# A hybrid decoder layer: gate and up projections as a 2x2 problem of half products, half of the chunk pairs in seven products, the rest plain

## The chip, the cores and the metric

The kernel runs on one core of one Trainium2 chip. The metric is the device time of one execution in microseconds (us), the median of the runs shown. A core has a matrix engine (TensorE, PE in the rows), three elementwise engines (VectorE or DVE, ScalarE or ACT, GpSimd or POOL), a queue that issues transfers (SyncE, SP), a memory of 128 partitions that the kernel manages (SBUF), and a memory in which products accumulate (PSUM); this kernel uses PSUM as eight tiles of 128x512 floats, called banks here, four for products (`mm`) and four for the rest (`aux`).

## The reference

256 tokens, width 2048, hidden width 5632, 32-bit floats throughout. The change is in the two feed-forward parts:

```python
def swiglu(h, w_gate, w_up, w_down):
    return (jax.nn.silu(h @ w_gate) * (h @ w_up)) @ w_down

x = x + 0.5 * swiglu(rms_norm(x, ffn1_norm[l]), ffn1_w_gate[l], ffn1_w_up[l], ffn1_w_down[l])
...  # gated linear attention beside block attention, w_in and w_out; a memory read with w_q, w_kv, w_o
x = x + 0.5 * swiglu(rms_norm(x, ffn2_norm[l]), ffn2_w_gate[l], ffn2_w_up[l], ffn2_w_down[l])
```

## The kernel before, in words

Every product is made from halves: an operand is split into `hi`, its rounding to the format fp32r, and `lo`, the rest. A product of 128 tokens x 128 rows x 512 columns is then three matmuls into one PSUM bank, hi x hi, hi x lo and lo x hi (L156, L157, L158). Weights stream from memory four 128-row chunks at a time (`load_raw`, 1 MB). `split_unit` splits them two chunks at a time: ScalarE writes `whi` (L130, 128x1024), then VectorE subtracts to get `wlo` (L131, 128x1024). `whi` and `wlo` have three buffers each, so a split waits until TensorE has read the buffer of three splits ago.

The activations `xhi` and `xlo` are the residual, transposed on TensorE (L223), multiplied by the gain (VectorE, L226) and split (ScalarE L228, VectorE L229); 1 / rms of a token is multiplied in behind the product. `Normed.block(j)` does this for one of four column blocks j and two token tiles.

`ffn` goes over 11 column blocks of 512 hidden columns in three runs (4, 4 and 3 blocks). For each column block it makes the gate product, 16 chunks x 2 token tiles x 3 = 96 matmuls into two banks, and the same for up; Silu of the gate (ScalarE, L275), times up (VectorE, L292), then a transpose and a split (L282, L196, L197; 8 transposes) for the down projection, which follows each run (L307 adds it to the residual). What runs behind the products (norms, transposes) is a queue of steps, one taken per product step by `pump()`. The order of instructions on each engine is made from this program by a scheduler before the run, and each engine takes its own in order.

Of the kernel before, what the change touches and what calls it, by code (L numbers as in the profile page):

```python
# [17 lines left out]
P = 128  # L18
# [26 lines left out]
OFF_MV = OFF_MK + BH * DH  # L45


@with_exitstack
def hymba_layer(ctx: ExitStack, tc: tile.TileContext, x, mem, ffn1_norm, ffn1_w_gate, ffn1_w_up,
# [27 lines left out]
    graw = tmp.tile([KC, P], F32, tag="S", name="graw", bufs=6)  # L77
# [12 lines left out]
    def turn_gains(src, dst):  # L90
        n = src.shape[0]
        ps = aux.tile([P, NB], F32, tag="aux", name=nm("aux"))
        nc.tensor.transpose(ps[:, :n], src, ident[:n, :n])
        nc.vector.tensor_copy(dst, ps[:, :n])

    turn_gains(graw, gT1)

    def aux_tile(shape):
        n = 1
        for s in shape[1:]:  # L100
            n *= s
# [7 lines left out]

    def tmp_tile(shape, tag, bufs=2, dtype=F32):  # L110
        return tmp.tile(shape, dtype, tag=tag, name=nm(tag), bufs=bufs)

    def half_kb(shape=(P, NB)):
        return tmp_tile(list(shape), "t2k", 8)
# [3 lines left out]
    def load_raw(k0, c0, w, n=NB, step=4):  # L118
        raw = wp.tile([P, 4, n], F32, tag="raw", name=nm("raw"))
        src = w[k0 * P:(k0 + 4) * P, c0:c0 + n].rearrange("(k p) n -> p k n", p=P)  # L120
        for k in range(0, 4, step):
            nc.sync.dma_start(raw[:, k:k + step, :], src[:, k:k + step, :])
        return raw

    def split_unit(raw, ks, n):
        got = []
        for k in ks:
            hi = wp.tile([P, 2, n], F32R, tag="whi", name=nm("whi"))
            lo = wp.tile([P, 2, n], F32R, tag="wlo", name=nm("wlo"))
            nc.scalar.activation(hi, raw[:, k:k + 2, :], AF.Copy)  # L130
            nc.vector.tensor_tensor(lo, raw[:, k:k + 2, :], hi.bitcast(F32), op=ALU.subtract)  # L131
            got += [(hi[:, i, :], lo[:, i, :]) for i in range(2)]
        return got

    class Block:
        """One [256 tokens, n columns] product; a step takes two or four 128-row chunks of it."""

        def __init__(self, a, w, c0, nk, done, w_k0=0, n=NB):
            self.a, self.w, self.c0, self.nk, self.w_k0, self.n = a, w, c0, nk, w_k0, n
            self.done = done  # L140
            self.ps = [mm.tile([P, NB], F32, tag="mm", name=nm("mm"))[:, :n] for _ in range(NT)]
            self.raw = {}

        def step(self, k0, nk=4):
            u, r = divmod(k0, 4)
            key = id(self.w), self.w_k0 + 4 * u, self.c0
            if u not in self.raw:
                self.raw[u] = ahead.pop(key) if key in ahead else load_raw(*key[1:], self.w, self.n)
            hi, lo = self.a
            ws = split_unit(self.raw[u], range(r, r + nk, 2), self.n)  # L150
            for t in range(NT):
                s = slice(t * P, (t + 1) * P)
                p = self.ps[t]
                for i, (wh, wl) in enumerate(ws):
                    k = k0 + i
                    nc.tensor.matmul(p, hi[:, k, s], wh, start=k == 0, stop=False)  # L156
                    nc.tensor.matmul(p, hi[:, k, s], wl, start=False, stop=False)  # L157
                    nc.tensor.matmul(p, lo[:, k, s], wh, start=False, stop=k == self.nk - 1)  # L158
# [19 lines left out]
    def run_blocks(specs, late=False, gap=4):  # L178
        """With late, the last chunks of the first two blocks come after the others of both."""
# [34 lines left out]
    def sumsq(src, dst):  # L214
        junk = tmp.tile([P, NB], BF16, tag="junk", name=nm("junk"), bufs=1)
# [3 lines left out]
    def norm_block(c, j, t, gi, hi, lo, ss):  # L219
        """Columns j of token tile t (c): transposed, times the gain, split; the squares summed."""  # L220
# [3 lines left out]
        xg = tmp_tile([P, 4, P], "xg")  # L224
# [614 lines left out]
```

## Time and profile before

| | |
|---|---|
| median of 3 runs | 1990.75 us (1989.64 to 1990.9) |
| profiled execution, first to last instruction (span) | 1987.1 us; the page gives no other time for it |
| TensorE matmuls busy | 1973.9 us, 99% |
| VectorE busy | 1075.3 us, 54% |
| ScalarE busy | 918.0 us, 46% |
| bytes moved | 369 MB, mean 186 GB/s |

A busy matmul is drawn as 0.39 us, but one starts every 0.2267 us, so that busy times of lines add up to more than the engine's. Of the elementwise engines, too, one instruction can start a little before the one ahead of it is drawn as ended: the distance of two starts is what an instruction takes from its queue.

### The profile page before, as it was taken

The numbers are of one execution on the slowest core, as the hardware profiler recorded it, in microseconds if no ns is written. First come the engines' busy times: TensorE is split into PE (matmuls) and PEld (weight loads), VectorE is DVE, ScalarE is ACT, GpSimd is POOL, SyncE is SP. The second block draws the span as 40 slices with busy tenths as digits, with TensorE's granted clock in tenths as the row PEclk, the third lists the DMA queues.
The fourth block names the chain that finished last, engine by engine and source line by source line (L and its number), as shares of the span: only waits on it lengthen the run. The fifth ranks groups of instructions, "written<-read, shape, count | busy, mean of one in ns | idle before, by whom it ended". The sixth has DMA issues, their size and how long they took to land.

```text
span 1987.1 us, 22549 instructions
## 1 busy us (share of the span) xinstructions
PE 1973.9 (99%) x9112; PEld 1640.8 (83%) x9112; DVE 1075.3 (54%) x1236; ACT 918.0 (46%) x1112; POOL 19.8 (1%) x52
## 2 busy tenths in 40 slices
PE   8999999999999999999999999999999999999999
PEld 6888888888888888987788889888888888888887
DVE  5454554445544465456665767655544444554444
ACT  5444434444344455635464656544433444434443
POOL 0000000000000000000000000000000000000000
PEclk9999999999999999999999999999999999999999
DMA  7655555555565556554455545555556555556554
GB/s 242 191 191 191 190 191 191 190 191 191 191 191 190 191 170 199 164 191 149 148 167 195 180 158 171 175 190 188 190 190 195 188 190 189 190 195 197 182 189 167
DMA packets 189857, 369.07 MB, mean 186 GB/s; under 512 B 6100, under 2 KB 16552, under 8 KB 189752
## 3 DMA queue, kind: packets, MB, share of 16 engines
q1 hardware_dynamic: 189752, 367.63, 56.7%
q8 instruction: 71, 1.16, 0.3%
q14 instruction: 34, 0.28, 0.0%
HBM read 365.50 MB, written 2.10 MB: 185 GB/s over the span
## 4 chain that ended last, share of the span: by engine, by line
PE 95%; issue 3%; DVE 1%; ACT 1%; DMA 0%; POOL 0%; SPq 0%; POOLq 0%; ACTq 0%
PE mm L157 31%; PE mm L156 30%; PE mm L158 30%; PE aux L282 1%; PE aux L223 1%; DVE wlo L131 0%; DMA x_sb<-in_x_dram 0%; PE aux L767 0%; PE aux L783 0%; PE aux L506 0%; ACT whi L130 0%; PE aux L639 0%; PE aux L585 0%; PE aux L535 0%; PE aux L517 0%
## 5 line engine op out<-in xcount | busy, mean ns | idle before, releaser
L131 DVE TENSOR_TENSOR wlo<-raw,whi 128x1024 fp32r<-128x1024 f32 (+3 forms) x704 | 847.1, 1205 | 852.1 <-ACT whi L130 823.6
L130 ACT ACTIVATE whi<-raw 128x1024 fp32r<-128x1024 f32 (+3 forms) x704 | 733.3, 1043 | 947.4 <-PE mm L158 946.2
L156 PE MATMUL mm<-whi,xhi 128*128 128x512 f32 (+2 forms) x1856 | 719.4, 388 | 0.1
L157 PE MATMUL mm<-wlo,xhi 128*128 128x512 f32 (+2 forms) x1856 | 716.8, 386 | 1.2 <-DVE wlo L131 1.2
L158 PE MATMUL mm<-whi,xlo 128*128 128x512 f32 (+2 forms) x1856 | 716.2, 386 | 0.0
L157 PEld LDWEIGHTS mm<-wlo,xhi 128*128 128x128 f32 x1856 | 348.9, 188 | 70.7 <-DVE wlo L131 3.1
L156 PEld LDWEIGHTS mm<-whi,xhi 128*128 128x128 f32 x1856 | 348.7, 188 | 70.3 <-issue 1.5
L158 PEld LDWEIGHTS mm<-whi,xlo 128*128 128x128 f32 x1856 | 348.7, 188 | 69.0 <-DVE xlo L229 0.2
L158 PE MATMUL mm<-whi,biglo 128*128 128x512 f32 x864 | 336.4, 390 | 0.0
L156 PE MATMUL mm<-whi,bighi 128*128 128x512 f32 x832 | 325.3, 391 | 0.0
L157 PE MATMUL mm<-wlo,bighi 128*128 128x512 f32 x832 | 324.0, 389 | 0.0
L158 PEld LDWEIGHTS mm<-whi,biglo 128*128 128x128 f32 x864 | 162.2, 188 | 33.9
L157 PEld LDWEIGHTS mm<-wlo,bighi 128*128 128x128 f32 x832 | 156.3, 188 | 32.1 <-DVE wlo L131 0.4
L156 PEld LDWEIGHTS mm<-whi,bighi 128*128 128x128 f32 x832 | 156.3, 188 | 31.8
L275 ACT ACTIVATE t2k<-mm,r 128x512 f32<-128x512 f32 x44 | 30.4, 692 | 40.4 <-PE mm L158 40.4
L307 DVE SCALAR_TENSOR_TENSOR x_sb<-mm,x_sb 128x512 f32<-128x512 f32 x48 | 33.0, 688 | 11.1 <-PE mm L158 11.0
L292 DVE SCALAR_TENSOR_TENSOR t2k<-mm,r,t2k 128x512 f32<-128x512 f32 x44 | 32.9, 748 | 8.1 <-PE mm L158 8.0
L197 DVE TENSOR_TENSOR biglo<-aux,bighi 128x512 fp32r<-128x512 f32 (+1 forms) x56 | 34.1, 645 | 0.0
L217 ACT ACTIVATE junk<-x_sb 128x512 bf16<-128x512 f32 x32 | 20.1, 627 | 19.2 <-DVE x_sb L307 9.9
L196 ACT ACTIVATE bighi<-aux 128x512 fp32r<-128x512 f32 (+1 forms) x56 | 28.8, 555 | 0.0
L226 DVE TENSOR_TENSOR xg<-aux,gT 128x512 f32<-128x512 f32 x40 | 25.7, 683 | 0.0
L282 PEld LDWEIGHTS aux<-ident,t2k 128*128 128x128 f32 x176 | 20.5, 141 | 2.9
(170 smaller groups left out, 643.8 us busy)
## 6 DMA issues: line engine op xcount, KB each, us to landing
raw<-in_ffn_w_up_dram SPq DMA_DIRECT2D x88, 1024.0 KB, 5.1
raw<-in_ffn_w_down_dram SPq DMA_DIRECT2D x88, 1024.0 KB, 4.9
raw<-in_ffn_w_gate_dram SPq DMA_DIRECT2D x87, 1024.0 KB, 5.1
raw<-in_w_in_dram SPq DMA_DIRECT2D x40, 1024.0 KB, 5.1
raw<-in_w_out_dram SPq DMA_DIRECT2D x16, 1024.0 KB, 4.9
raw<-in_w_in_dram SPq DMA_DIRECT2D x8, 688.0 KB, 4.2
raw<-in_xattn_w_kv_dram SPq DMA_DIRECT2D x4, 1024.0 KB, 4.9
raw<-in_xattn_w_q_dram SPq DMA_DIRECT2D x4, 1024.0 KB
```

The source lines that it names most:

```text
L130: nc.scalar.activation(hi, raw[:, k:k + 2, :], AF.Copy)
L131: nc.vector.tensor_tensor(lo, raw[:, k:k + 2, :], hi.bitcast(F32), op=ALU.subtract)
L156: nc.tensor.matmul(p, hi[:, k, s], wh, start=k == 0, stop=False)
L157: nc.tensor.matmul(p, hi[:, k, s], wl, start=False, stop=False)
L158: nc.tensor.matmul(p, lo[:, k, s], wh, start=False, stop=k == self.nk - 1)
L196: nc.scalar.activation(hi, src, AF.Copy)
L197: nc.vector.tensor_tensor(lo, src, hi.bitcast(F32), op=ALU.subtract)
L226: nc.vector.tensor_tensor(xg, pt, g[:, :, None].to_broadcast([P, 4, P]), op=ALU.mult)
L275: nc.scalar.activation(sg[b, t], ps[t], AF.Silu, scale=a.rstd[:, t:t + 1])
L282: nc.tensor.transpose(pt[:, i, :], h[t][:, i * P:(i + 1) * P], ident)
L292: nc.vector.scalar_tensor_tensor(h[t], ps[t], a.rstd[:, t:t + 1], sg[b, t], op0=ALU.mult, op1=ALU.mult)
L307: nc.vector.scalar_tensor_tensor(c, ps[t], 0.5, c, op0=ALU.mult, op1=ALU.add)
```

## The change

Let x0, x1 be the two token tiles (the rows of the 2x2 problem) and two neighbouring chunks the inner dimension; the columns are gate and up. For the first four of the eight chunk pairs of a column block (`KINDS` "S"), the eight half products x_t,k times gate_k or up_k are replaced by seven (the scheme of Strassen in Winograd's form): on the weight side VectorE makes four sums of 128x512 (`sa`, `sb`), on the activation side four differences per pair, once for all column blocks. Each of the seven is three matmuls into a bank of its own: `p1`, `r6`, `r7`, `p2`, `r5`, `r3`, `q4`. For the last four pairs ("N") eight plain half products go into four of the same banks, two of them as one with the difference of both token tiles (`dh`, `dl`), as 24 matmuls. `early`, `gates` and `ups` put the banks together on VectorE. So a column block has 4 x 21 + 4 x 24 = 180 matmuls.

With seven banks for `mm` one is left for `aux` in the feed-forward parts. Pools for PSUM and scratch are opened for three phases (`a`, `b`, `c`). Weights come two chunks per transfer (512 KB) into five buffers; `whi` and `wlo` have five buffers in the feed-forward parts. The mixer's constants are made at the start of phase `b`.

```diff
+RAWS = 5
+HIS = 5
+T2K = 7
+KINDS = "SSSSNNNN"
...
-    def load_raw(k0, c0, w, n=NB, step=4):
-        raw = wp.tile([P, 4, n], F32, tag="raw", name=nm("raw"))
...
+    def load_raw(k0, c0, w, n=NB):
+        raw = wp.tile([P, 2, n], F32, tag="raw", name=nm("raw"))
+        nc.sync.dma_start(raw, w[k0 * P:(k0 + 2) * P, c0:c0 + n].rearrange("(k p) n -> p k n", p=P))
+        return raw
...
+    def split_raw(raw, n=NB):
+        bufs = 3 if "mix" in pools else HIS
+        hi, lo = (tmp_tile([P, 2, n], tag, bufs, F32R) for tag in ("whi", "wlo"))
+        split_to(hi, lo, raw)
+        return [(hi[:, i, :], lo[:, i, :]) for i in range(2)]
+
+    def mm3(p, a, w, start, stop):
+        nc.tensor.matmul(p, a[0], w[0], start=start, stop=False)
+        nc.tensor.matmul(p, a[0], w[1], start=False, stop=False)
+        nc.tensor.matmul(p, a[1], w[0], start=False, stop=stop)
...
+        def step(self, q):
...
+            g = take_raw(2 * q, self.c0, self.wg)
+            u = take_raw(2 * q, self.c0, self.wu)
+            if KINDS[q] == "N":
+                gs, us = split_raw(g), split_raw(u)
+                for name, t, ws in (("p2", 0, gs), ("q4", 1, gs), ("r3", None, us), ("r5", 1, us)):
+                    for i, w in enumerate(ws):
+                        x = a.diff(2 * q + i) if t is None else a.plain(t, 2 * q + i)
+                        self.add(name, x, w, i == 1)
+            else:
+                sa, sb = (tmp_tile([P, 2, NB], "st") for _ in range(2))
+                nc.vector.tensor_tensor(sa[:, 0, :], g[:, 0, :], u[:, 0, :], op=ALU.add)
+                nc.vector.tensor_tensor(sa[:, 1, :], u[:, 0, :], u[:, 1, :], op=ALU.add)
+                nc.vector.tensor_tensor(sb[:, 0, :], sa[:, 0, :], u[:, 1, :], op=ALU.add)
+                nc.vector.tensor_tensor(sb[:, 1, :], sb[:, 0, :], g[:, 1, :], op=ALU.add)
+                hu, lu = (tmp_tile([P, NB], tag, 2, F32R) for tag in ("hu", "lu"))
+                gs = split_raw(g)
+                split_to(hu, lu, u[:, 1, :])
+                sums = split_raw(sa) + split_raw(sb)
+                e, o = 2 * q, 2 * q + 1
+                for name, x, w in (("p1", a.plain(0, e), gs[0]), ("p2", a.plain(0, o), gs[1]),
+                                   ("r3", a.comb(3, q), (hu, lu)),
+                                   ("r5", a.comb(0, q), sums[0]), ("r7", a.comb(2, q), sums[1]),
+                                   ("r6", a.comb(1, q), sums[2]), ("q4", a.plain(1, o), sums[3])):
+                    self.add(name, x, w, True)
+            pump()
+
+        def early(self):
+            self.p1, self.v2, self.v3 = half_kb(), half_kb(), half_kb()
+            nc.scalar.activation(self.p1, self.p["p1"], AF.Copy)
+            nc.vector.tensor_tensor(self.v2, self.p["r6"], self.p1, op=ALU.subtract)
+            nc.vector.tensor_tensor(self.v3, self.p["r7"], self.v2, op=ALU.add)
...
+            nc.vector.tensor_tensor(c, self.p["p2"], self.p1, op=ALU.add)
...
+            nc.vector.tensor_tensor(c, self.p["q4"], self.v3, op=ALU.subtract)
...
+            nc.vector.tensor_tensor(c, self.p["r5"], c, op=ALU.add)
+            nc.vector.tensor_tensor(c, self.p["r3"], c, op=ALU.add)
...
+            nc.vector.tensor_tensor(c, self.p["r5"], c, op=ALU.add)
...
+        def sums(self, q, x):
+            f = tmp_tile([P, 4, P], "xg", 3)
+            if KINDS[q] == "S":
+                for out, x0, x1 in ((f[:, 0], x[1][:, 0], x[1][:, 1]),
+                                    (f[:, 1], x[0][:, 0], f[:, 0]),
+                                    (f[:, 2], x[1][:, 0], x[0][:, 0]),
+                                    (f[:, 3], x[0][:, 1], f[:, 1])):
+                    nc.vector.tensor_tensor(out, x0, x1, op=ALU.subtract)
+                i = self.s.index(q)
+                split_to(self.e[0][:, i], self.e[1][:, i], f)
+            else:
+                f = f[:, :2]
+                nc.vector.tensor_tensor(f, x[0], x[1], op=ALU.subtract)
+                i = self.n.index(q)
+                split_to(self.d[0][:, i], self.d[1][:, i], f)
...
+    phases = [phase("a", 7)]
...
+    next_phase("b", 4)
...
+    next_phase("c", 7)
```

VectorE's queue where one column block of the first feed-forward part ends and the next begins, before: `wlo` are splits of weights, L292 multiplies gate and up (one per token tile), `biglo` splits the transposed result.

```order
L131 TENSOR_TENSOR wlo_825<-raw_822,whi_824 128x1024
L292 SCALAR_TENSOR_TENSOR t2k_816<-mm_678,r_300,t2k_674 128x512
L131 TENSOR_TENSOR wlo_829<-raw_822,whi_828 128x1024
L292 SCALAR_TENSOR_TENSOR t2k_817<-mm_679,r_300,t2k_676 128x512
L131 TENSOR_TENSOR wlo_873<-raw_870,whi_872 128x1024
L131 TENSOR_TENSOR wlo_877<-raw_870,whi_876 128x1024
L131 TENSOR_TENSOR wlo_907<-raw_904,whi_906 128x1024
L197 TENSOR_TENSOR biglo_184<-aux_856,bighi_183 128x4x128
```

The same queue and place after the change. `st_3129` and `st_3130` are `sa` and `sb` of the new block's second S pair, L243 to L253 put the old block's banks (`mm_2697` to `mm_2700`) together, L422 is what L292 was.

```order
L143 TENSOR_TENSOR wlo_3094<-st_3076,whi_3093 128x1024
L243 TENSOR_TENSOR t2k_3053<-mm_2697,t2k_2903 128x512
L246 TENSOR_TENSOR t2k_3055<-mm_2700,t2k_2905 128x512
L219 TENSOR_TENSOR st_3130<-st_3129,raw_3127 128x512
L143 TENSOR_TENSOR wlo_3138<-raw_3125,whi_3137 128x1024
L220 TENSOR_TENSOR st_3130<-st_3130,raw_3125 128x512
L252 TENSOR_TENSOR t2k_2904<-mm_2698,t2k_2904 128x512
L256 TENSOR_TENSOR t2k_2905<-mm_2698,t2k_2905 128x512
L253 TENSOR_TENSOR t2k_2904<-mm_2699,t2k_2904 128x512
L422 SCALAR_TENSOR_TENSOR t2k_2905<-t2k_2905,r_353,t2k_3055 128x512
L422 SCALAR_TENSOR_TENSOR t2k_2904<-t2k_2904,r_353,t2k_3053 128x512
L143 TENSOR_TENSOR wlo_3144<-st_3129,whi_3143 128x1024
```

The first S pair of the new block (`wlo_3094` is its last split) and the splits of the second's gate stand ahead of the old block's end; the sums' splits of the second pair (`wlo_3144`) stand behind it.

VectorE's queue after the change, at the start of the second feed-forward part: between the blocks of the product with `w_o` (L871 adds one to the residual) stand the norm (`xg`, `xlo`), and now its differences (L364) and their split (`el`).

```order
L143 TENSOR_TENSOR xlo_10492<-xg_10503,xhi_10491 128x4x128
L364 TENSOR_TENSOR xg_10520<-xg_10514 128x128
L364 TENSOR_TENSOR xg_10520<-xg_10514,xg_10503 128x128
L364 TENSOR_TENSOR xg_10520<-xg_10503,xg_10520 128x128
L220 TENSOR_TENSOR st_10696<-st_10696,raw_10691 128x512
L143 TENSOR_TENSOR xlo_10492<-xg_10514,xhi_10491 128x4x128
L364 TENSOR_TENSOR xg_10520<-xg_10503,xg_10520 128x128
L871 TENSOR_TENSOR x_sb<-mm_10536,x_sb 128x512
L871 TENSOR_TENSOR x_sb<-mm_10537,x_sb 128x512
L143 TENSOR_TENSOR el_10495<-xg_10520,eh_10494 128x512
L143 TENSOR_TENSOR wlo_10704<-raw_10691,whi_10703 128x1024
```

Before, the same place reads as follows (L733 is now L871; `xg`, `xlo` and `wlo` alone stand between).

```order
L733 TENSOR_TENSOR x_sb<-mm_9276,x_sb 128x512
L226 TENSOR_TENSOR xg_9365<-aux_9360,gT_89 128x512
L226 TENSOR_TENSOR xg_9376<-aux_9371,gT_89 128x512
L131 TENSOR_TENSOR wlo_9449<-raw_9446,whi_9448 128x1024
L229 TENSOR_TENSOR xlo_9358<-xg_9365,xhi_9357 128x4x128
L229 TENSOR_TENSOR xlo_9358<-xg_9376,xhi_9357 128x4x128
L733 TENSOR_TENSOR x_sb<-mm_9384,x_sb 128x512
```

VectorE's queue where the first feed-forward part ends and the mixer's product with `w_in` begins, before: a first split for `w_in` (128x704) stands ahead of the last two additions to the residual (L307).

```order
L131 TENSOR_TENSOR wlo_5148<-raw_5145,whi_5147 128x704
L307 SCALAR_TENSOR_TENSOR x_sb<-mm_5005,x_sb 128x512
L131 TENSOR_TENSOR wlo_5152<-raw_5145,whi_5151 128x704
L307 SCALAR_TENSOR_TENSOR x_sb<-mm_5006,x_sb 128x512
```

After the change all of them stand behind both additions (L430), since the scratch pool of phase `b` takes the place of that of phase `a`.

```order
L143 TENSOR_TENSOR xlo_5745<-xg_5959,xhi_5744 128x4x128
L430 SCALAR_TENSOR_TENSOR x_sb<-mm_5905,x_sb 128x512
L430 SCALAR_TENSOR_TENSOR x_sb<-mm_5906,x_sb 128x512
L143 TENSOR_TENSOR wlo_6094<-raw_6091,whi_6093 128x704
L143 TENSOR_TENSOR wlo_6112<-raw_6109,whi_6111 128x704
```

## Rows read from the trace of the kernel before

**Rows 1.** The page: busy time by engine; TensorE's granted clock in 40 slices, tenths

```profile
PE 1973.9 (99%) x9112; PEld 1640.8 (83%) x9112; DVE 1075.3 (54%) x1236; ACT 918.0 (46%) x1112; POOL 19.8 (1%) x52
...
PEclk9999999999999999999999999999999999999999
```

**Rows 2.** One column block: busy time by engine, clock, DMA share, GB/s

```profile
320.90:365.30 44.40, 44.40 (x201) 36.84 (x201) 22.12 (x20) 19.25 (x20) 0.00 (x0) 1.00 0.59 189
```

**Rows 3.** Timeline of TensorE: start, duration, instruction; six starts apart

```profile
56.67 0.39 PE L156 MATMUL mm<-whi,xhi 128*128 128x512 f32 x1
...
58.03 0.39 PE L156 MATMUL mm<-whi,xhi 128*128 128x512 f32 x1
```

**Rows 4.** Timeline of VectorE: the first token tile's product in two neighbouring column blocks

```profile
320.92 0.75 DVE L292 SCALAR_TENSOR_TENSOR t2k<-mm,r,t2k 128x512 f32<-128x512 f32 x1 [0.40 <-PE mm L158]
...
365.34 0.75 DVE L292 SCALAR_TENSOR_TENSOR t2k<-mm,r,t2k 128x512 f32<-128x512 f32 x1 [0.40 <-PE mm L158]
```

**Rows 5.** Groups by line and shape: busy us, mean ns | idle before, releaser

```profile
L131 DVE TENSOR_TENSOR wlo<-raw,whi 128x1024 fp32r<-128x1024 f32 x664 | 815.6, 1229 | 824.3 <-ACT whi L130 796.1
L130 ACT ACTIVATE whi<-raw 128x1024 fp32r<-128x1024 f32 x664 | 704.9, 1062 | 923.3 <-PE mm L158 922.4 <-DMA raw<-in_ffn_w_gate_dram 0.5 <-PE aux L93 0.3
...
L292 DVE SCALAR_TENSOR_TENSOR t2k<-mm,r,t2k 128x512 f32<-128x512 f32 x44 | 32.9, 748 | 8.1 <-PE mm L158 8.0
...
L578 DVE TENSOR_TENSOR t2k<-t2k,r 128x512 f32<-128x512 f32 x12 | 8.2, 687 | 0.2
```

**Rows 6.** Timeline of VectorE where its queue never waits (x2: two as one row)

```profile
1240.26 1.28 DVE L733 TENSOR_TENSOR x_sb<-mm,x_sb 128x512 f32<-128x512 f32 x2
1241.46 1.28 DVE L226 TENSOR_TENSOR xg<-aux,gT 128x512 f32<-128x512 f32 x2
1242.65 1.22 DVE L131 TENSOR_TENSOR wlo<-raw,whi 128x1024 fp32r<-128x1024 f32 x1
1243.79 1.29 DVE L229 TENSOR_TENSOR xlo<-xg,xhi 128x512 fp32r<-128x512 f32 x2
```

**Rows 7.** Waits: engine and line, for whom, us in total, times, longest

```profile
ACT whi L130 <- PE mm L158: 946.2, 621, 3.9
...
PE mm L157 <- DVE wlo L131: 1.2, 2, 0.8
```

**Rows 8.** Timeline of VectorE: its first split, and the first block's two products

```profile
7.64 1.23 DVE L131 TENSOR_TENSOR wlo<-raw,whi 128x1024 fp32r<-128x1024 f32 x1 [6.70 <-ACT whi L130]
...
56.41 0.75 DVE L292 SCALAR_TENSOR_TENSOR t2k<-mm,r,t2k 128x512 f32<-128x512 f32 x1
...
59.78 0.74 DVE L292 SCALAR_TENSOR_TENSOR t2k<-mm,r,t2k 128x512 f32<-128x512 f32 x1
```

**Rows 9.** Timeline of VectorE: first addition behind w_o; first block's product, second feed-forward part

```profile
1237.54 1.28 DVE L733 TENSOR_TENSOR x_sb<-mm,x_sb 128x512 f32<-128x512 f32 x2
...
1296.27 0.75 DVE L292 SCALAR_TENSOR_TENSOR t2k<-mm,r,t2k 128x512 f32<-128x512 f32 x1
```

**Rows 10.** Timeline of VectorE: from the first feed-forward part to the mixer

```profile
743.34 0.69 DVE L307 SCALAR_TENSOR_TENSOR x_sb<-mm,x_sb 128x512 f32<-128x512 f32 x1 [0.90 <-PE mm L158]
745.59 0.89 DVE L131 TENSOR_TENSOR wlo<-raw,whi 128x704 fp32r<-128x704 f32 x1 [1.55 <-ACT whi L130]
746.39 0.68 DVE L307 SCALAR_TENSOR_TENSOR x_sb<-mm,x_sb 128x512 f32<-128x512 f32 x1
```

**Rows 11.** Groups by line and shape: small shapes on VectorE

```profile
L197 DVE TENSOR_TENSOR biglo<-aux,bighi 128x256 fp32r<-128x256 f32 x8 | 3.2, 418 | 0.0
...
L602 DVE TENSOR_SCALAR t2k<-t2k,sums 128x128 f32<-128x128 f32 x8 | 2.3, 286 | 0.3
```

**Rows 12.** The chain that ended last: eight transposes of one column block

```profile
329.04 0.87 PE aux L282 x8
```

**Rows 13.** Timeline of TensorE at its start

```profile
13.02 0.63 PE L158 MATMUL mm<-whi,xlo 128*128 128x512 f32 x1
13.45 0.63 PE L156 MATMUL mm<-whi,xhi 128*128 128x512 f32 x1
```

More of the change, by code (lines that the diff above doesn't have):

```diff
@@ L140, in __init__ @@
             self.done = done
-            self.ps = [mm.tile([P, NB], F32, tag="mm", name=nm("mm"))[:, :n] for _ in range(NT)]
-            self.raw = {}
+            self.ps = [bank(n) for _ in range(NT)]
         def step(self, k0, nk=4):
[L145 to L148, printed above, removed]
             hi, lo = self.a
[L150 to L158, printed above, removed]
+            for k2 in range(k0, k0 + nk, 2):
+                ws = split_raw(take_raw(self.w_k0 + k2, self.c0, self.w, self.n), self.n)
+                for t in range(NT):
+                    s = slice(t * P, (t + 1) * P)
+                    for i, w in enumerate(ws):
+                        k = k2 + i
+                        mm3(self.ps[t], (hi[:, k, s], lo[:, k, s]), w, k == 0, k == self.nk - 1)
             pump()
@@ L247, in block @@
         def block(self, j):
-            if self.a is None:
+            if self.hi is None:
                 self.begin()
-            for t in range(NT):
-                norm_block(x_sb[:, t, j * NB:(j + 1) * NB], j, t, self.gi, *self.a, self.ss)
+            x = [norm_block(x_sb[:, t, j * NB:(j + 1) * NB], j, t, self.gi, self.hi, self.lo,
+                            self.ss) for t in range(NT)]
+            if self.pairs:
+                for q in (2 * j, 2 * j + 1):
+                    self.sums(q, [y[:, 2 * q - 4 * j:2 * q - 4 * j + 2, :] for y in x])
@@ L255, in behind, with plain, comb, diff @@
+        def plain(self, t, k):
+            s = slice(t * P, (t + 1) * P)
+            return self.hi[:, k, s], self.lo[:, k, s]
+        def comb(self, c, q):
+            return tuple(e[:, self.s.index(q), c] for e in self.e)
+        def diff(self, k):
+            return tuple(d[:, self.n.index(k // 2), k % 2] for d in self.d)
         def behind(self, j):
@@ L313, in ffn, with next_phase @@
                        late=True)
-    n1 = Normed(G1)
+    phases = [phase("a", 7)]
+    phases[0].__enter__()
+    def next_phase(name, n_mm):
+        phases.pop().__exit__(None, None, None)
+        phases.append(phase(name, n_mm))
+        phases[0].__enter__()
+    turn_gains(graw, gT1)
+    n1 = Normed(G1, True)
     def load_x(j):
@@ L325, in start, with load_ahead @@
             yield
-    ahead[id(w1g), 0, 0] = load_raw(0, 0, w1g, step=2)
+    def load_ahead(k0):
+        for w in (w1g, w1u):
+            ahead[id(w), k0, 0] = load_raw(k0, 0, w)
+    load_ahead(0)
     load_x(1)
-    ahead[id(w1g), 4, 0] = load_raw(4, 0, w1g)
+    load_ahead(2)
     load_x(2)
     load_x(3)
-    ahead[id(w1g), 8, 0] = load_raw(8, 0, w1g)
     n1.block(0)
@@ L692, in __init__ @@
         def __init__(self, tags):
-            self.parts = [act_tile([P, 8, M], t, F32R) for t in tags]
+            self.parts = [own_tile([P, 8, M], t, F32R) for t in tags]
         def __getitem__(self, i):
```

199 lines of the change are left out of this document (116 added, 83 removed).

## The prediction

> **What bounds the kernel now.** Read the page's busy shares first: TensorE has matmuls in 99% of the span, VectorE is busy in 54%, and the clock is granted in full in every slice [rows 1]. So look at one column block of gate and up: 44.40 us, TensorE busy throughout, VectorE 22.1 us and ScalarE 19.3 us of it [rows 2]; the same point of the next block follows 44.42 us later [rows 4]. A matmul starts every (58.03 - 56.67) / 6 = 0.2267 us [rows 3]. 192 of them are 43.52 us, and eight transposes 0.87 [rows 12], together 44.4: the block is TensorE's queue and nothing else. The waits agree: ScalarE's splits wait 946 us for TensorE to free a buffer, while TensorE's products wait 1.2 us in all for VectorE's splits [rows 7]. VectorE has 22 us to spare in each block. The change spends that spare time.
>
> **What an instruction of VectorE costs.** The group view draws a 128x512 instruction with two tensors as 687 ns, a 128x1024 split as 1229 and the product with Silu as 748 [rows 5]. In a full queue they start closer than that: two additions and then two norm products start 0.60 apart (1240.26 to 1241.46 for two, 1241.46 to 1242.65 for two), a split takes 1.14 (1242.65 to 1243.79), and two `xlo`, with both operands in SBUF as the new sums have them, are 1.29 together, so the second began 0.60 after the first [rows 6]. My prices are therefore 0.60 for 512 wide, 1.14 for 1024 and 0.67 for L422 (0.75 less the same 0.08). Upper bound: the durations, 0.69, 1.23 and 0.75. Lower bound: 1.14 - 0.60 = 0.54 for 512 columns alone and 1.08 for 1024, with no gap left between two instructions.
>
> A rule of the Trainium skill speaks for the upper bound: "VectorE: DVE Perf Modes", section "The DRAIN you can't avoid", says that the next operation does not start until the pipe is empty. By it a column block would have 46.0 us of VectorE where my prices give 41.5. The rows, 0.60 against 0.69, don't bear it out, and the same section grants that an instruction that is not held starts earlier.
>
> **The change, per column block.** TensorE: 180 matmuls x 0.2267 = 40.81 us in place of 43.52, so 2.72 less, 59.8 over 22 blocks if nothing else waits. VectorE: an S pair has four sums, one 512-wide split and three 1024-wide ones, 5 x 0.60 + 3 x 1.14 = 6.42 us, where its 21 matmuls take 4.76. An N pair has two splits, 2.28, against 24 matmuls, 5.44. Putting banks together (seven instructions), the two L422 and two `biglo` are 7 x 0.60 + 2 x 0.67 + 2 x 0.60 = 6.74. Sum 4 x 6.42 + 4 x 2.28 + 6.74 = 41.5 us beside TensorE's 40.81 + 0.87 = 41.7. Two engines of equal load, coupled by five buffers, do not run at 41.7: VectorE is short in the S pairs and stopped by full buffers in the N pairs.
>
> How far, is found by laying the instructions out along a loop. Start where TensorE begins the first N pair. (1) The last N pair's up split reuses the buffer of the second N pair's gate, free after 24 + 12 matmuls, 8.16 us. (2) The end of the last matmul lies 0.16 behind its slot; then ScalarE splits (1.06, [rows 5]), VectorE subtracts (1.14), with 0.17 of hand-over: 2.53. (3) VectorE goes on without a stop through the next block's S pairs and the old block's end, in the order shown: up to the third sum of the last S pair 25 x 0.60 + 9 x 1.14 + 2 x 0.67 = 26.6, with 0.2 of small waits 26.8. (4) The last S pair: a split 1.14, a sum and a small split 1.20, two splits, the second after 0.47 since ScalarE's copy of `p1` stands ahead of its half, 1.14 + 0.47 + 1.28; then TensorE's last six matmuls, 1.36: 6.59. Sum 8.16 + 2.53 + 26.8 + 6.59 = 44.1 us, 0.3 below the 44.4 of now. With the upper prices 39 instructions of the loop take about 0.09 more each, 47.5; with the lower ones it is 43.1. TensorE waits some 2.4 us per block, all of it in S pairs.
>
> **The four first blocks of later runs** (two in each part). At their start no old block is put together: five instructions that join banks, two L422 and two `biglo`, 5.5 us, fall out of the queue ahead of the S pairs, and two additions to the residual, 1.2, stand there. VectorE is 4.3 us further on than in the loop, more than the 2.4 waited there, so these blocks take TensorE's time: -2.72 each, -10.9.
>
> **The two first blocks of a part.** Here the norm and its differences share VectorE with the first four S pairs. Up to the first N split its queue has, in the first part, 40 instructions of 512, 13 of 1024, 8 of 256 (0.33), 16 of 128 (0.20; both durations less 0.09, [rows 11]) and 9 small ones: 24.0 + 14.8 + 2.6 + 3.2 + 1.7 = 46.3 us. It starts at 7.64 as now [rows 8]; I add 3 us for the chains through ScalarE and the single `aux` bank, so the N pairs begin at 57 and end 96 x 0.2267 = 21.8 later, at 78.8. Now this block ends 2.7 us (12 matmuls) behind 56.4, at 59.1 [rows 8]. +19.7. In the second part the queue from the first addition behind `w_o` (1237.54) has 48, 14, 8, 16 and 7: 52 us; 1237.5 + 52 + 3 + 21.8 = 1314.3 against 1296.3 + 2.7 = 1299.0 [rows 9]: +15.3. Bounds: no stall at all, -6 for both; twice 3 us more, +6.
>
> **The phases.** Today a split for `w_in` lies between the two last additions [rows 10]; afterwards ScalarE's half waits for TensorE's last matmul and VectorE's for both additions. TensorE waits for 0.6 + 0.9 to 2.6 us; I take 2 for each of two changes of phase, +4.
>
> **Edits at nothing.** ScalarE has 20 wide splits per block in place of 16, four half as wide and the copy of `p1`: 19.3 + 4 x 1.06 + 4 x 0.6 + 0.7 = 27 us, well under the block's 44. The bytes are the same, at 0.59 of the DMA engines [rows 2]; halved transfers are twice as many issues, about one per 2.7 us on SP's queue, which has no other work there. If a transfer came late, a wait of about as many us per block would follow. The mixer's constants move onto GpSimd and the queue of `w_in`'s weights, behind five loads.
>
> **Sum.** 16 other blocks x (44.1 - 44.4) = -5.3; first blocks of runs -10.9; first blocks of parts +35.0; phases +4. Together +22.8: a span of 1987.1 + 22.8 = 2010, and 3.6 us more around it (1990.75 against 1987.1), **2014 us**. With the bounds of the first blocks and of the phases, and 0.6 us either way per block, 2003 to 2032 for this case.
>
> **Rivals.**
> *Durations are the price* (no overlap in so mixed a queue): 16 x 3.1 + 35 + 14 (some 160 instructions x 0.09) - 10.9 + 4 = +92, 2083 us. For it: nearly each new instruction hangs on a semaphore; against it: those of rows 6 do, too. Half of that: 2050. (By the Trainium skill, "VectorE: DVE Perf Modes", "The DRAIN you can't avoid", this case would be the rule.)
> *TensorE stays the bound* (the other side): if the loop's 33 us of VectorE were 2.4 shorter, each block would take 41.7: 16 x -2.7 - 10.9 + 35 + 4 = -15, 1975 us. It decides from 1.4 us (4%) off that chain: starts and phases less the runs' first blocks cost 39 - 10.9 = 28 us, 1.76 for each of 16 blocks, so blocks of 42.65 break even. For it: the scheduler already moves the next pair's sums ahead of the old block's end; against it: the rows show no price that low but the bare 0.54.
> *No change*: the lower prices, 43.1 per block, and first blocks without stalls and with them cheaper, 16 x -1.3 - 10.9 + 25 + 4: -2, 1988.
> *The clock*: at its start TensorE's matmuls are 0.43 apart [rows 13], the lower level (1.2 GHz), later 0.2267 with 1.00 granted throughout. In the first block it would have 19 us of products in 47. If waits in S pairs brought the lower level back for one N pair in each of 18 blocks, 24 x 0.2 = 4.9 us each, 2014 + 88 = 2102.
>
> **How the numbers follow.** This measurement can tell about 0.2%, 4 us. Main case 0.64; half the durations 0.06; full durations 0.08; clock 0.05; no change 0.09; TensorE the bound 0.08. Slower by over 0.2%: 0.64 + 0.06 + 0.08 + 0.05 = 0.83; within 0.09; faster 0.08. The range 1990 to 2062 takes in the main case, the halfway one and most of no change: 0.79.
>
> **What would show it.** Right: VectorE over 90% busy in column blocks; 44 us from block to block, with TensorE's waits in the S pairs on `wlo` and none in the N pairs; first N pair at about 57 us; 41 us for the first block of a later run. Wrong: starts of VectorE 0.69 apart (upper price), blocks of 41.7 (the sums hidden), or a granted clock under 1 beyond the first block.

## The result, and the profile after

| | before | after |
|---|---|---|
| median | 1990.7 us (1989.64 to 1990.9) | 2019.0 us (2018.6 to 2019.15) |
| ratio | | 1.0144 (1.013 to 1.0159) |
| span of the profiled execution | 1987.1 us | 2017.4 us |

The kernel became 1.4% slower: +30.3 us of span where +22.8 were forecast. The page of after, to be laid beside [rows 1], has 457 us more of VectorE and a TensorE that is no longer always busy. One run of the version with a sixth raw buffer came out slow (2061.6 us, at a mean granted clock of 0.918) and is left out of its time below.

```profile
PE 1966.3 (97%) x8848; PEld 1588.0 (79%) x8848; DVE 1531.9 (76%) x1974; ACT 1061.7 (53%) x1326; POOL 23.5 (1%) x52
...
PEclk8999999999999999999999999899999999999999
```

Busy time by engine in four stretches of after (the columns are those of [rows 2]): the first block's S pairs; a whole block of the loop; N pairs; S pairs.

```profile
12.00:57.00 45.00, 35.27 (x118) 25.45 (x118) 44.39 (x85) 29.82 (x48) 0.00 (x0) 0.85 0.39 126
81.56:126.01 44.45, 43.66 (x190) 34.05 (x189) 42.03 (x53) 25.88 (x30) 0.00 (x0) 1.00 0.59 190
363.00:387.00 24.00, 24.00 (x107) 19.74 (x106) 20.12 (x24) 12.36 (x15) 0.00 (x0) 1.00 0.67 219
78.60:100.60 22.00, 21.21 (x91) 15.63 (x90) 21.91 (x28) 14.03 (x18) 0.00 (x0) 1.00 0.45 139
```

Read it by stretches: VectorE is full in the S pairs (21.91 of 22.00) while TensorE waits, and TensorE is full in the N pairs (24.00 of 24.00) while VectorE has time. Over a block the two look nearly equal. The clock is below 1 only in the first block of each part, where VectorE is full: 0.85 in the first row above, 0.91 in the second part from the additions behind `w_o` to its first N pair (the second 8 of the page's row):

```profile
1258.00:1312.00 54.00, 45.38 (x186) 33.60 (x186) 53.28 (x96) 35.44 (x57) 0.00 (x0) 0.91 0.34 104
```

VectorE's full queue, start, duration and instruction, in an S pair: starts 0.60 and 1.14 apart, though the instructions are drawn as 0.69 and 1.22 long, as in [rows 6].

```profile
112.93 0.69 DVE L218 TENSOR_TENSOR st<-raw 128x512 f32<-128x512 f32 x1
113.53 0.69 DVE L219 TENSOR_TENSOR st<-st,raw 128x512 f32<-128x512 f32 x1
114.13 1.22 DVE L143 TENSOR_TENSOR wlo<-raw,whi 128x1024 fp32r<-128x1024 f32 x1
115.27 0.69 DVE L220 TENSOR_TENSOR st<-st,raw 128x512 f32<-128x512 f32 x1
```

L237 runs once per block, just behind the first N split. It is the clock hand of the loop; first its places in the first block of each part, then four in a row.

```profile
56.12 0.69 DVE L237 TENSOR_TENSOR t2k<-mm,t2k 128x512 f32<-128x512 f32 x1
...
1310.03 0.69 DVE L237 TENSOR_TENSOR t2k<-mm,t2k 128x512 f32<-128x512 f32 x1
...
318.88 0.69 DVE L237 TENSOR_TENSOR t2k<-mm,t2k 128x512 f32<-128x512 f32 x1
362.67 0.69 DVE L237 TENSOR_TENSOR t2k<-mm,t2k 128x512 f32<-128x512 f32 x1
408.66 0.69 DVE L237 TENSOR_TENSOR t2k<-mm,t2k 128x512 f32<-128x512 f32 x1
453.24 0.69 DVE L237 TENSOR_TENSOR t2k<-mm,t2k 128x512 f32<-128x512 f32 x1
```

All 16 such distances in the two parts lie between 43.74 and 45.99, mean 44.51. The first block of a later run is read on TensorE, from its first matmul to the first of the block behind it: 341.09 - 300.03 = 41.06 us for 180 matmuls. The other three are alike: in all four L237 starts 19.11 us behind the last pair of additions of the run before.

```profile
300.03 0.39 PE L154 MATMUL mm<-whi,xhi 128*128 128x512 f32 x1
...
341.09 0.39 PE L154 MATMUL mm<-whi,xhi 128*128 128x512 f32 x1
```

The waits (engine and line, for whom, us in total, times, longest) show what is late. TensorE, and its weight loads (PEld), wait for the splits in S pairs, more for `whi` than for `wlo`, since ScalarE's split of a sum has to wait for VectorE's sum (L218, L220). The splits also wait for transfers, 148 us with 3.5 for `w_down` (before: 0.5 for the gate's weights, [rows 5]). Of these, 131 us end within 16 us behind L237, while TensorE has its N pairs and the other two engines already work on the next block's S pairs (`hu`, `st`).

```profile
ACT hu L142 <- DMA raw<-in_ffn_w_up_dram: 59.7, 40, 3.1
ACT whi L142 <- DVE st L218: 59.2, 39, 3.8
PEld mm L154 <- ACT whi L142: 38.7, 44, 3.1
ACT whi L142 <- DMA raw<-in_ffn_w_up_dram: 38.0, 25, 2.7
ACT whi L142 <- DVE st L220: 35.2, 32, 1.7
ACT whi L142 <- DMA raw<-in_ffn_w_gate_dram: 23.9, 17, 2.1
PEld mm L155 <- DVE wlo L143: 23.1, 50, 2.9
DVE st L217 <- DMA raw<-in_ffn_w_up_dram: 22.9, 20, 2.0
```

Three more places of VectorE: two additions behind `down`, 96 matmuls apart; the last addition of the first part ([rows 10]); the first behind `w_o` ([rows 9]).

```profile
541.74 1.28 DVE L430 SCALAR_TENSOR_TENSOR x_sb<-mm,x_sb 128x512 f32<-128x512 f32 x2
563.77 1.28 DVE L430 SCALAR_TENSOR_TENSOR x_sb<-mm,x_sb 128x512 f32<-128x512 f32 x2
763.95 0.69 DVE L430 SCALAR_TENSOR_TENSOR x_sb<-mm,x_sb 128x512 f32<-128x512 f32 x1 [0.69 <-PE mm L156]
1257.74 1.28 DVE L871 TENSOR_TENSOR x_sb<-mm,x_sb 128x512 f32<-128x512 f32 x2
```

### The profile page after: what moved, and what is told of

The parts are those of the page before. It is cut to its first block, busy times and chain, and to the rows that moved or that the text cites. A ratio compares the mean times of both kernels' runs of the same rounds, so it can differ in the third digit from the quotient of the medians.

```text
span 2017.4 us, 24213 instructions
## 1 busy us (share of the span) xinstructions
PE 1966.3 (97%) x8848; PEld 1588.0 (79%) x8848; DVE 1531.9 (76%) x1974; ACT 1061.7 (53%) x1326; POOL 23.5 (1%) x52
## 4 chain that ended last, share of the span: by engine, by line
PE 77%; DVE 16%; ACT 2%; issue 2%; DMA 2%; ACTq 0%; SPq 0%; DVEq 0%
PE mm L154 25%; PE mm L155 25%; PE mm L156 24%; DVE wlo L143 7%; ACT whi L142 2%; DVE st L217 1%; DMA raw<-in_ffn_w_up_dram 1%; DVE st L218 1%; DVE t2k L422 1%; DVE st L219 1%; DVE st L220 1%; DVE lu L143 1%; PE aux L315 1%; DVE biglo L143 0%; DVE xlo L143 0%
## 5 line engine op out<-in xcount | busy, mean ns | idle before, releaser
L143 DVE TENSOR_TENSOR wlo<-raw,whi 128x1024 fp32r<-128x1024 f32 (+3 forms) x616 | 732.6, 1200 | 389.6 <-ACT whi L142 388.8
L155 PE MATMUL mm<-wlo,xhi 128*128 128x512 f32 (+2 forms) x1240 | 485.0, 391 | 3.7 <-DVE wlo L143 3.7
L154 PE MATMUL mm<-whi,xhi 128*128 128x512 f32 (+2 forms) x1240 | 482.7, 393 | 1.0 <-ACT whi L142 1.0
L156 PE MATMUL mm<-whi,xlo 128*128 128x512 f32 (+2 forms) x1240 | 480.2, 387 | 0.0
L155 PEld LDWEIGHTS mm<-wlo,xhi 128*128 128x128 f32 x1240 | 234.4, 189 | 53.1 <-DVE wlo L143 10.5
L154 PEld LDWEIGHTS mm<-whi,xhi 128*128 128x128 f32 x1240 | 234.0, 189 | 48.8 <-ACT whi L142 2.1
L156 PEld LDWEIGHTS mm<-whi,xlo 128*128 128x128 f32 x1240 | 234.3, 189 | 47.1
L142 ACT ACTIVATE whi<-st 128x1024 fp32r<-128x1024 f32 x176 | 185.8, 1059 | 130.2 <-DVE st L218 59.2
L143 DVE TENSOR_TENSOR wlo<-st,whi 128x1024 fp32r<-128x1024 f32 x176 | 212.6, 1220 | 6.2 <-ACT whi L142 5.0
L155 PE MATMUL mm<-wlo,eh 128*128 128x512 f32 x264 | 106.8, 405 | 2.5 <-DVE wlo L143 1.0
L217 DVE TENSOR_TENSOR st<-raw,raw 128x512 f32<-128x512 f32 x88 | 60.6, 688 | 23.7 <-DMA raw<-in_ffn_w_up_dram 22.9
```

The source lines that it names most:

```text
L154: nc.tensor.matmul(p, a[0], w[0], start=start, stop=False)
L155: nc.tensor.matmul(p, a[0], w[1], start=False, stop=False)
L156: nc.tensor.matmul(p, a[1], w[0], start=False, stop=stop)
L217: nc.vector.tensor_tensor(sa[:, 0, :], g[:, 0, :], u[:, 0, :], op=ALU.add)
```

## The experiments

The theory: VectorE's queue sets the time in two places, through a row of four S pairs in every block, and in the first block of a part, where norm and differences come on top. The rivals: transfers through five buffers; the banks, phases and half transfers; the clock. Ratios are against the kernel before, timed on the same chip, with their 95% interval.

### The sums left out

```diff
-                sa, sb = (tmp_tile([P, 2, NB], "st") for _ in range(2))
-                nc.vector.tensor_tensor(sa[:, 0, :], g[:, 0, :], u[:, 0, :], op=ALU.add)
...
-                sums = split_raw(sa) + split_raw(sb)
+                sums = split_raw(g) + split_raw(u)
```

> Leaves out the four weight sums of each S pair (the sums' splits read the raw weights in their place, so the values are not those of the layer); every split, matmul, bank and transfer stays. Theory (VectorE's queue through the S pairs sets the loop of 44.5 us): an S pair drops from 6.42 to 4.02 us of VectorE, under TensorE's 4.76, so blocks come every 41.7 to 42.3 us, 16 x -2.4 = -38, and each first block of a part is 16 x 0.6 = 9.6 us shorter, -19: about 1960 us. Rival (transfers through five raw buffers set the loop): blocks stay at 44 to 44.5, only the first blocks gain: about 2000. Rival (seven banks and one aux bank, or the phases, are the cost): 2000 or more.

1961.8 us, ratio 0.9856 (0.9841 to 0.9871). VectorE's end of a block (its product with Silu, two token tiles in a row) comes every 41.98 us:

```profile
369.99 1.41 DVE L417 SCALAR_TENSOR_TENSOR t2k<-t2k,r,t2k 128x512 f32<-128x512 f32 x2
411.97 1.40 DVE L417 SCALAR_TENSOR_TENSOR t2k<-t2k,r,t2k 128x512 f32<-128x512 f32 x2
```

Same transfers, banks, splits and matmuls; 2.4 us of VectorE less in each S pair, and the loop is TensorE's. The theory holds for the loop, and both rivals fall as its main cause.

### A sixth raw buffer

```diff
+        if "mix" not in pools:
+            pools["x6"] += 1
+            if pools["x6"] % 6 == 0:
+                raw = tmp_tile([P, 2, n], "rawx", 1)
...
         return load_raw(k0, c0, w, n)
```

> A sixth raw weight buffer in both feed-forward parts, nothing else. If late transfers in the N pairs are what lifts the loop from 44.1 to 44.5 us: waits of the splits on transfers fall from some 120 us in all to under half, loop 44.1, about -7 us, 2012. Rival (the transfers are late only because VectorE frees buffers late, so that one more buffer fills and nothing moves): within 2 us of 2019.

2014.0 us, ratio 1.0118 (1.0097 to 1.0138); this overlaps the interval of the change itself, 1.013 to 1.0159. The trace is clearer: the mean of the 16 loops is 44.10 us, and the waits for feed-forward weights are down to 71 us, most of them these (L225 is L217 there):

```profile
ACT hu L150 <- DMA raw<-in_ffn_w_up_dram: 22.1, 26, 1.6
DVE st L225 <- DMA raw<-in_ffn_w_up_dram: 19.1, 10, 3.0
DVE st L225 <- DMA rawx<-in_ffn_w_up_dram: 15.3, 8, 2.6
ACT hu L150 <- DMA rawx<-in_ffn_w_up_dram: 11.6, 12, 1.7
```

So late transfers cost the loop at least 0.4 us per block, 6.6 in all; 71 us of waits are left. A transfer reuses the raw buffer of five transfers ago, and lands 3.9 to 4.6 us after it is issued (median by tensor); in N pairs, where they are used up fastest, that is too late.

### S and N in turn

```diff
-KINDS = "SSSSNNNN"
+KINDS = "SNSNSNSN"
```

> The same eight pairs with S and N in turn (SNSNSNSN): the same instructions on every engine. Theory (VectorE is short in a row of four S pairs and stopped by full buffers in four N pairs): S and N together are 6.42 + 2.28 = 8.7 us of VectorE against 10.2 of TensorE, so only the old block's end (6.74) piles up: blocks of 42 to 43 us, 16 x -2 = -32, and each first block of a part about 9 us shorter, since N pairs' products run while VectorE works on later chunks: about 1970 us. Rival (loads are equal, 41.5 against 41.7, and durations or transfers decide, not the order): blocks stay at 44 or more, 2010 to 2020. Prediction's rival (TensorE stays the bound at 41.7) would give 1960.

1978.5 us, ratio 0.9943 (0.9928 to 0.9958). One block of it:

```profile
377.04:418.66 41.62, 41.62 (x188) 34.17 (x187) 41.54 (x52) 24.98 (x29) 0.00 (x0) 1.00 0.65 203
```

The same instructions as in the change, with both engines full for the whole block. So it was not VectorE's sum that cost 3 us per block but where it lay: a row of S pairs makes VectorE late, a row of N pairs gives the time back too late. The end of the first block (L422) moved from 81.56 to 71.42, but the second block took 47.2. That VectorE carried over what it had not done is likely, and not shown.

### The first block of each part plain

```diff
+            if plain:
+                self.p = {n: bank() for n in ("p2", "q4", "r3", "r5")}
...
-            if KINDS[q] == "N":
+            if self.plain or KINDS[q] == "N":
...
-                for name, t, ws in (..., ("r3", None, us), ...):
+                for name, t, ws in (..., ("r3", 0 if self.plain else None, us), ...):
...
-                pair = Pair(a, wg, wu, b * NB)
+                pair = Pair(a, wg, wu, b * NB, b == 0)
```

> The first column block of each part is made plain (eight half products in four banks, 192 matmuls, no weight sums, no banks to join), the activation differences still made in it for the later blocks. Theory (the first block's excess of 18.8 and 12.6 us is VectorE's queue of norm, differences, sums and splits): both go back to their old length within 2 us, about -29, 1990 us. Rival (it is the clock, granted at 0.85 there, or the norm's chain through the single aux bank): less than a third of it comes back, 2010 or more.

1985.9 us, ratio 0.9978 (0.9968 to 0.9987): 33.5 us less of span than the change, for two blocks of 22. In the window to be laid beside the first of after:

```profile
12.00:60.00 48.00, 47.22 (x212) 38.48 (x212) 43.69 (x78) 33.48 (x49) 0.00 (x0) 1.00 0.71 228
```

The norm and its differences still stand there; TensorE hardly waits, and the clock is granted in full. So the first blocks' excess came from the sums and their splits on top of the norm, and the clock of 0.85 went with TensorE's waits: VectorE, full there (44.39 of 45.00), was what held the block, not the clock.

### All blocks plain

```diff
-                pair = Pair(a, wg, wu, b * NB)
+                pair = Pair(a, wg, wu, b * NB, True)
...
-    n1 = Normed(G1, True)
+    n1 = Normed(G1)
...
-    n4 = Normed(G2, True)
+    n4 = Normed(G2)
```

> Every column block plain in four of the seven banks (192 matmuls, no weight sums, no activation differences, nothing to join), with the change's phases, its one aux bank, half transfers, five buffers and constants in phase b. Theory (these cost only the two changes of phase): blocks of 44.4 us as before, 1993 us, 1990 to 1996. Rival (the single aux bank, the phases or the half transfers are a good part of the +28): 2000 or more.

2007.8 us, ratio 1.0087 (1.007 to 1.0104). The rival's number came out, and none of its three reasons shows as a wait inside the blocks. The splits wait 0.3 us in all for gate and up weights, and TensorE is busy throughout, but a block takes 44.85 us instead of 44.42, because all its matmuls stand further apart: 38 distances in the second pair of rows are 8.69 us, 0.2287 each, where before they are 0.2267 ([rows 3]).

```profile
372.23 1.41 DVE L430 SCALAR_TENSOR_TENSOR t2k<-mm,r,t2k 128x512 f32<-128x512 f32 x2
417.08 1.40 DVE L430 SCALAR_TENSOR_TENSOR t2k<-mm,r,t2k 128x512 f32<-128x512 f32 x2
...
324.26 0.39 PE L154 MATMUL mm<-whi,xhi 128*128 128x512 f32 x1
...
332.95 0.39 PE L156 MATMUL mm<-whi,xlo 128*128 128x512 f32 x1
```

The change has it, too: 0.2281 over the 180 matmuls from 300.03, and 22.03 / 96 = 0.2295 in `down` between 541.74 and 563.77. Of the 18 us of span that this run has more than the kernel before, 22 blocks x 0.43 and 2112 matmuls of `down` x 0.0022 are 14 (an estimate). Another 2.6 lie between the first part and `w_o`, as in the change.

### Both orders together, and two tries with GpSimd

The next run joins the two edits above.

> SNSNSNSN in all column blocks but the first of each part, which is plain. Theory (a row of S pairs and the first blocks are two separate places where VectorE holds TensorE back): the 28 us that the plain first blocks gave beyond what turning the order gave there, less the 2.7 us more of TensorE in each, come on top: about 1952 us, 1945 to 1958. Rival (both draw on the same slack of VectorE, and the differences just hold up the second block): 1968 or more.

1962.8 us, ratio 0.9865 (0.985 to 0.988): 16 below the order alone, between theory (26) and rival (10 or less). Each edit by itself had also relieved the first block, so part of the gain was counted twice. In the blocks behind, both engines are full:

```profile
366.70:408.10 41.40, 41.37 (x186) 33.85 (x185) 41.40 (x52) 25.60 (x29) 0.00 (x0) 1.00 0.65 203
```

Two of the sums on the idle GpSimd, with the change's own order:

```diff
-                nc.vector.tensor_tensor(sa[:, 1, :], u[:, 0, :], u[:, 1, :], op=ALU.add)
+                nc.gpsimd.tensor_tensor(sa[:, 1, :], u[:, 0, :], u[:, 1, :], op=ALU.add)
...
-                nc.vector.tensor_tensor(sb[:, 1, :], sb[:, 0, :], g[:, 1, :], op=ALU.add)
+                nc.gpsimd.tensor_tensor(sb[:, 1, :], sb[:, 0, :], g[:, 1, :], op=ALU.add)
```

> Two of the four weight sums of each S pair (the second and the fourth) on GpSimd, which is idle there; order SSSSNNNN and all else as in the change. Theory (VectorE's instructions alone set the loop): 1.2 us less of VectorE per S pair, 4.8 per block, so TensorE's 41.7 to 42.5 bounds the loop: 16 x -2.2, and 5 less in each first block, about 1974 us. Rival (an addition of GpSimd takes some 1.6 us, half of the 3.17 of its 128x1024 product, and comes late for the split behind it, or VectorE is slower beside it): blocks stay at 44 or longer, 2015 or more.

2074.7 us, ratio 1.0422 (1.0401 to 1.0443), blocks of some 47 us. The group view by shape shows both halves of the rival at once: GpSimd's sums take 2.0 us, and VectorE's instructions beside them grow, its third sum from 685 ns in the change to 927, the sums' splits from 1220 to 1510.

```profile
L218 POOL TENSOR_TENSOR st<-raw 128x512 f32<-128x512 f32 x88 | 180.3, 2049 | 1026.6 <-DMA raw<-in_ffn_w_up_dram 649.2 <-DVE wlo L143 191.1 <-DMA raw<-in_ffn_w_gate_dram 186.3
...
L143 DVE TENSOR_TENSOR wlo<-st,whi 128x1024 fp32r<-128x1024 f32 x176 | 263.3, 1510 | 6.5 <-ACT whi L142 5.3
...
L219 DVE TENSOR_TENSOR st<-st,raw 128x512 f32<-128x512 f32 x88 | 81.6, 927 | 0.6
```

How they grow is seen in one S pair (start, duration), first on GpSimd, then on VectorE:

```profile
369.21 2.21 POOL L218 TENSOR_TENSOR st<-raw 128x512 f32<-128x512 f32 x1 [1.76 <-DVE wlo L143]
373.84 1.62 POOL L220 TENSOR_TENSOR st<-st,raw 128x512 f32<-128x512 f32 x1 [2.42 <-ACT whi L142]
...
370.19 0.68 DVE L143 TENSOR_TENSOR biglo<-aux,bighi 128x512 fp32r<-128x512 f32 x1
370.79 1.18 DVE L217 TENSOR_TENSOR st<-raw,raw 128x512 f32<-128x512 f32 x1
...
374.24 3.57 DVE L143 TENSOR_TENSOR wlo<-st,whi 128x1024 fp32r<-128x1024 f32 x2
```

L217 ends at 371.97, 0.55 behind GpSimd's end at 371.42, as if it had started only there; the two splits take 1.2 us more than their usual 2.36, and GpSimd works for 1.22 of that time (374.24 to 375.46). So while GpSimd adds, a VectorE instruction with both inputs in SBUF stands; `biglo`, with one input in PSUM, takes its 0.60 beside it.

By the Trainium skill, "SBUF — State Buffer", section "Who interferes with whom", a VectorE instruction with two inputs in SBUF contends with a GpSimd instruction that reads SBUF, and the port pair that they share is an exclusive lock. The trace agrees (1.2 us more on two splits, beside 1.22 of GpSimd).

GpSimd's sums together with both orders:

> SNSNSNSN, first block of each part plain, and the second and fourth weight sum on GpSimd. Theory: VectorE at 36.7 us per block has slack everywhere, every block goes at TensorE's 41.7 to 42: 5 to 12 us below the same without GpSimd, 1938 to 1947. Rival (GpSimd's sums are late or slow VectorE): above it, 1955 or more.

2039.1 us, ratio 1.0243 (1.0222 to 1.0263): 76 us worse than the same without GpSimd. Its mean granted clock was 0.988 (1.000 without GpSimd), so a part of the 76 may be the clock's; that part was not measured.

### What sets the distance of matmuls

Three runs asked for it. By the addresses in the two programs, every large tile of the change starts 32 bytes behind a multiple of 64; before, on one. So the kernel before was shifted, and the change padded back:

```diff
-    gT1 = const.tile([P, KC], F32, name="gT1")
+    gT1 = const.tile([P, KC + 8], F32, name="gT1")[:, :KC]
```

> The kernel before, with one constant (the first gains) 32 bytes longer, so that every large tile behind it in SBUF starts at 32 instead of 0 modulo 64 bytes, as in the change; nothing else. Theory (a matmul whose operands start there takes 0.2289 us instead of 0.2267, the pitch that all kernels with the change show, in the mixer and the down products too): 9112 x 0.0022 = 20 us slower, about 2010 us. Rival (the pitch comes from the change of bank every six matmuls instead of twelve, from five buffers or from half transfers): 1990 us, no change.

```diff
-    gT2 = const.tile([P, 4 * KC + 4], F32, name="gT2")
+    gT2 = const.tile([P, 80], F32, name="gT2")[:, :4 * KC + 4]
```

> The change, with the other gains' tile padded to 320 bytes, so that the large tiles start at 0 modulo 64 bytes again; nothing else. Theory (addresses set the pitch of matmuls): 0.2267 us everywhere; it counts where TensorE is the bound: 4888 matmuls outside the column blocks, four first blocks of runs, and some 42 matmuls of each loop, 4888 x 0.0022 + 4 x 180 x 0.0018 + 18 x 42 x 0.0018 = 13.4 us less, about 2005 us. Rival (order, buffers or transfers set it): 2017 to 2021.

1989.8 us, ratio 1.0 (0.999 to 1.0009), and 2016.5 us, ratio 1.0131 (1.0114 to 1.0148). The theory of addresses modulo 64 falls: the shifted kernel keeps 0.2267 (15 distances are 3.40 us),

```profile
500.05 0.39 PE L156 MATMUL mm<-whi,bighi 128*128 128x512 f32 x1
...
503.45 0.39 PE L156 MATMUL mm<-whi,bighi 128*128 128x512 f32 x1
```

and in the padded one two additions behind `down` stand 22.02 us apart (540.59 and 562.61), as in the change. All edits together but GpSimd's:

> SNSNSNSN, first block of each part plain, a sixth raw buffer and the padding. Theory: against 1962.8 without the last two, 8872 x 0.0019 = 17 us for the pitch, since TensorE bounds nearly everything there, and some 3 us of late transfers: about 1943 us, 1938 to 1948. Rival (VectorE bounds the column blocks there, too, or the addresses do nothing): 1953 or more.

1961.6 us, ratio 0.9858 (0.9843 to 0.9873), the rival's number: padding and sixth buffer add nothing there. Last, on top of these, twelve matmuls per bank in the other products:

```diff
+            ws = []
             for k2 in range(k0, k0 + nk, 2):
-                ws = split_raw(take_raw(self.w_k0 + k2, self.c0, self.w, self.n), self.n)
-                for t in range(NT):
...
+                ws += split_raw(take_raw(self.w_k0 + k2, self.c0, self.w, self.n), self.n)
+            for t in range(NT):
```

> The run before (SNSNSNSN, first block plain, sixth raw buffer, padding) with one edit in the down, mixer and memory products: twelve matmuls into one bank, then twelve into the other, as in the kernel before, instead of six and six; transfers of 512 KB and all buffers stay. Theory (the change's matmuls are 0.2289 us apart because the bank changes twice as often): those some 4600 matmuls go back to 0.2267, about -10 us, 1951. Rival (the half transfers or another part of the change set the pitch): 0.2289 stays, 1960 to 1963.

1961.0 us, ratio 0.9862 (0.9845 to 0.988), no change; 15 distances in `down` are 3.43 us, 0.2287 each.

```profile
500.23 0.39 PE L162 MATMUL mm<-whi,bighi 128*128 128x512 f32 x1
...
503.66 0.39 PE L162 MATMUL mm<-whi,bighi 128*128 128x512 f32 x1
```

So the order of banks in these products is not it either. One thing the traces do show: the extra time hangs on the operands. In `down` the three matmuls of one chunk differ, three after three: behind `whi` x `bighi` the next starts after 0.2313 us on average, behind `wlo` x `bighi` after 0.2268, behind `whi` x `biglo` after 0.2289 (before: 0.2267, 0.2266, 0.2268). Products with `dh` have 0.2267 in the change, too. The three go into one bank and come from the same transfers and buffer counts, which points to where in SBUF the operands lie. That, half transfers and the number of buffers were not tried by themselves; the cause stays open.

## Why the prediction was right, and where it was off

| term | forecast | measured |
|---|---|---|
| 16 other blocks | -5.3 | 16 x (44.51 - 44.42) = +1.4 |
| first blocks of later runs | -10.9 | 4 x (41.06 - 43.52) = -9.8 |
| first blocks of parts | +35.0 | 18.8 + 12.6 = +31.4 |
| mixer and phases | +4 | 20.2 - 17.6 = +2.6 |
| `down` | 0 | 2112 x 0.0022 = +4.6 (estimate) |
| sum | +22.8 | +30.2, of +30.3 |

The terms miss by +6.7, +1.1, -3.6, -1.4 and +4.6 us, so that 2014 came so near to 2019 is in part luck. So is the agreement of the sum to 0.1: read at TensorE's first product with `dh` in each block, the 16 distances average 44.44, which takes 1 us away.

- **VectorE's price** was right: 0.60 and 1.14 from start to start. The rival of full durations falls. The rule of the Trainium skill beside it, "VectorE: DVE Perf Modes", section "The DRAIN you can't avoid", does not hold as a price for these queues: 0.60 against a drawn 0.69. The section excepts instructions that are not held.
- **The loop**: the chain was right but for one link (TensorE waits more for the sums' `whi` than for `wlo`), and its 44.1 came out once a sixth buffer stood (44.10). To the digit this is luck: 71 us of late transfers and the wider distance of matmuls are still in it. With five buffers it is 44.51. The step that failed is the edit at nothing for the DMA: its condition (if a transfer comes late, about as much per block) was written down, and it came true, though not one for one: 77 us of waits less gave back 0.4 us per block, 6.6 in all. The forecast weighed the load, 0.59 of the DMA engines over a block; the place where it mattered is the N pairs, 0.67 and 219 GB/s against 0.45 and 139 in the S pairs, with buffers for five transfers only.
- **First blocks of parts**: +18.8 (the N pairs began at 56.1, forecast 57, and end 21.8 later at 77.9 against 59.1) and +12.6 (1310.03 + 21.8 = 1331.8 against 1299.0 is +32.8, of which 20.2 stood at the first addition behind `w_o` already). The cause is shown by the run with plain first blocks; the N pairs began 0.9 us and, counted from `w_o`, 2.7 us earlier than forecast, so the 3 us for chains, or VectorE's count, were somewhat too much.
- **First blocks of later runs**: 41.06, forecast 41.
- **Phases**: 2.6 from 763.95 - 746.39 = 17.6 to 1257.74 - 1237.54 = 20.2, and that holds the mixer's wider distance of matmuls, too. The version with all blocks plain has the same 2.6. The two changes of phase cost less than the 4 us taken.
- **TensorE's price** was the step that failed without a warning: 0.2267 was carried over from the kernel before to every matmul of the new one. It became 0.228 to 0.229 on average. Where VectorE's chain sets the time this is hidden; in `down` it is 4.6 us (an estimate).
- **Rivals**: "TensorE stays the bound" was named with its condition, 2.4 us per block off VectorE's chain. Leaving the sums out did that and gave 1961.8 where it had 1975 (there the sums' time is gone from the first blocks, too). Turning the order did it without leaving out anything.
- **The clock** was low in the first block of each part, in its S pairs, and never in an N pair, so the rival of 2102 falls. The sign that was named against the forecast, a clock under 1 beyond the first block, did come in the second part (0.91), but in a stretch that VectorE filled (53.28 of 54.00).

The best version, with S and N in turn and a plain first block, takes 1961 to 1963 us, 1.4% below the kernel before. The seven products pay here when VectorE's work for them is spread out and kept away from the norm.

## What to carry to other kernels

When a change moves work from the bound engine to one with time to spare, lay both queues out stretch by stretch: equal sums per block (41.5 and 41.7) still cost 3 us when one engine's work lies in the first half and the other's in the second, and nothing when heavy and light steps alternate. Look apart at the first step of each part, where the spare engine has other work; a plain first step there is cheap (2.7 us of TensorE each, against 31 us for both). And carry no engine's pace over unseen: a version with everything but the idea (all blocks plain) shows what the rest of the change costs, here 17 us.

## What the runs showed of the hardware that was not expected

- The same 128x512 matmul starts every 0.2267 us in the kernel before and every 0.228 to 0.229 in all versions of the change, on average, at a granted clock of 1.00. Start addresses modulo 64 and the bank order don't set it. It differs between operands within one kernel: 0.2313, 0.2268 and 0.2289 in turn in `down`, and in the product with `w_kv` the change has 1.40 us for six with `s8b` and `s8d`, 0.233 each.

```profile
1171.00 0.39 PE L155 MATMUL mm<-wlo,s8b 128*128 128x512 f32 x1
...
1172.40 0.40 PE L155 MATMUL mm<-wlo,s8b 128*128 128x512 f32 x1
```

- A 128x512 addition takes 2.0 us on GpSimd beside a busy VectorE, and VectorE's instructions with both inputs in SBUF stand still meanwhile: help from an idle engine cost 56 us (2074.7 against 2019.0).
